# Six buffers of rounded weights moved to six different starts within 256 bytes

## The chip, the cores and the metric

The kernel runs on 1 core of a Trainium2 chip. The metric is the device time of one execution in microseconds; the median of three executions is quoted, and one further execution was recorded by the hardware profiler.

## What is computed

One residual decoder block on 512 tokens of width 2048, in fp32. Each sub-layer is normed and modulated by six vectors (shift, scale, gate, twice) that come from a conditioning vector `c`:

```python
mod = einsum('bd,de->be', silu(c), w_ada) + b_ada
h   = rms_norm(x, norm1) * (1 + sc1) + sh1
u, v, xb, gb = split(einsum('bsd,de->bse', h, w_in))
ya  = gmlp_spatial_gating(gelu(u), gelu(v), ...)
yb  = rg_lru(causal_dwconv(xb), ...) * gelu(gb)
mix = concat([rms_norm(ya), rms_norm(yb)])
x   = x + g1 * einsum('bse,ed->bsd', mix, w_out)
h   = rms_norm(x, norm2) * (1 + sc2) + sh2
gate, val = split(einsum('bsd,df->bsf', h, w_up))
x   = x + g2 * einsum('bsf,fd->bsd', gelu(causal_dwconv(gate)) * val, w_down)
out = rms_norm(x, norm_final)
```

The four weight products (`w_in`, `w_out`, `w_up`, `w_down`) are nearly all of the work.

## The kernel before

Weights arrive in blocks of 256 rows by 512 columns, each a tile of 128 partitions by 2 by 512 floats, 4096 bytes in each partition (`raw`, `rawb` or `t`). TensorE multiplies in fp32r. To keep fp32 precision, each weight block and each activation is held as two fp32r tiles: the rounded value, and the rest that rounding left out. Three matmuls then make one product: rounded times rounded, rounded weight times the activation's rest, and the weight's rest times the rounded activation.

The work is a list of 516 steps, one for each weight block. At step j, `round_step(j + 2)` has ScalarE cast the block of step j + 2 into a tile `wh` (`round_up`, L161 to L164) and `rest_step(j + 2)` has VectorE subtract it from the raw block into a tile `wl` (`rest`, L166 to L169); then TensorE runs the matmuls of step j. So weights are rounded two steps ahead, and three buffers of each kind (`WBUFS = 3`) turn over: one in use, one ready, one being written. The order of every engine's work is written out by hand (a manual schedule), with other work attached to steps by `put`.

Two kinds of step matter here. In 208 of them (`mm_w`, L171 to L176, and `mm_h`, L178 to L183) a step has 24 matmuls of 512 columns, in threes; each loads its own 128 x 128 stationary tile. In `mm_w` that tile is a slice of `wh` or `wl`, and the activation (`hp`, `dp`, `xs`) streams; in `mm_h` it is the other way round. The other 308 steps (`product`, L904 to L922) compute most of the up projection by a scheme of seven products of half size: each step has 8 pairs, one matmul of 512 columns with a slice of `wh` (L921) and one of 256 columns with a slice of `wl` (L922).

SBUF has two stacks of pools. The pool `weights` with the six buffers is the lowest of the left stack; above it stand in turn `mid`, `early`, `late`, `spare`, `ffn` and `back`, with `araw`, `yl`, `rawb`, `t`, `ht`, `la`, `dp` and others. The right stack (`main`) holds `hp`, `raw`, `xs` and constants. In the built program the six buffers start at bytes 1152, 5248 and 9344 (`wh`) and 13440, 17536 and 21632 (`wl`) of a partition. All six leave a remainder of 128 when divided by 256, and so do `hp`, `xs`, `dp`, `raw`, `rawb`, `t`, `yl` and most other large tiles. The constant tile `ones` starts at a remainder of 32; `ht`, `wst`, `wr`, `wi` and, in the stretch of the recurrent unit, `la` and `lc` start at 192 (`la` of a later pool also at 0); the four `araw` tiles at 128, 160, 192 and 224.

Of the kernel before, what the change touches and what calls it, by code (L numbers as in the profile page):

```python
# [9 lines left out]
F32 = mybir.dt.float32  # L10
F32R = mybir.dt.float32r
# [4 lines left out]
P = 128  # L16
S = 512
# [14 lines left out]
NMM = 6  # L32
NXS = 24
WBUFS = 3


ROUNDS = [(0, 2), (2, 6), (6, 10), (10, 16)]
# [13 lines left out]
def tile_block(ctx, tc, x_t, vec, w_ada, w_in, w_r, w_i, ws_t, w_out, w_up, w_us, w_dn, out):  # L51
# [3 lines left out]
    wts = ctx.enter_context(tc.tile_pool(name="weights", bufs=1))  # L55
# [5 lines left out]
    def sb(tag, bufs, shape=(P, S), dt=F32, pl=pool):  # L61
        count[0] += 1
        return pl.tile(list(shape), dt, name=f"{tag}_{count[0]}", tag=tag, bufs=bufs)
# [94 lines left out]
            put(j, fn, cost, half)  # L158


    def round_up(raw):  # L161
        hi = sb("wh", WBUFS, (P, 2, S), F32R, wts)
        A.copy(hi, raw)  # L163
        return hi  # L164

    def rest(raw, hi):  # L166
        lo = sb("wl", WBUFS, (P, 2, S), F32R, wts)
        V.tensor_tensor(out=lo, in0=raw, in1=hi, op=SUB)  # L168
        return [(hi[:, kk, :], lo[:, kk, :]) for kk in range(2)]  # L169

# [98 lines left out]
    def round_step(j):  # L269
        if j < len(steps):  # L270
            if j in source:
                raws[j] = source[j]()
            his[j] = round_up(raws[j])

    def rest_step(j):
        if j < len(steps):
            ws[j] = rest(raws.pop(j), his.pop(j))
# [1021 lines left out]
```

## Time and profile before

| | |
|---|---|
| median of 3 executions | 2104.73 us (2103.9 to 2104.93) |
| the profiled execution | 2104.92 us, of which the span from first to last instruction is 2103.2 us |
| granted TensorE clock, mean | 0.993 of full speed |
| TensorE matmul busy | 2069.0 us (98%), 10160 instructions |
| TensorE weight load busy | 1727.6 us (82%), 10160 instructions |
| VectorE busy | 1492.9 us (71%) |
| ScalarE busy | 923.8 us (44%) |
| GpSimd busy | 79.7 us (4%) |

Busy time of an engine is the sum of its instructions' durations, overlaps counted once. Matmuls are pipelined: a matmul's recorded duration includes the time in which its successor already streams, so the pace of TensorE is read from the distance between starts, not from durations.

### The profile page before, as it was taken

To read this page: it belongs to the slowest core of one execution; us is meant where nothing else is said; L and a number is where in the kernel's file an instruction comes from. 1 tells how busy PE (TensorE), PEld (TensorE's weight loads), DVE (VectorE), ACT (ScalarE), POOL (GpSimd) and SP (SyncE) were. 2 spreads that over 40 slices of the span, in tenths; PEclk is the share of its full clock that TensorE was granted. 3 is DMA by queue.
4 is the path that set the end of the run, shared out by engine and by line. 5 is a ranking of instruction groups with operands and counts; after the bars stand their busy time and mean duration, and the time that the engine had idled before them with its cause. 6 is when DMAs were issued, how large, how long until landed. Compare 5 with 4: busy or idle time off the path is not lost.

```text
span 2103.2 us, 26309 instructions
## 1 busy us (share of the span) xinstructions
PE 2069.0 (98%) x10160; PEld 1727.6 (82%) x10160; DVE 1492.9 (71%) x1865; ACT 923.8 (44%) x1165; POOL 79.7 (4%) x100
## 2 busy tenths in 40 slices
PE   7999999999989999999999999999999999999997
PEld 4887777888868888888888888888888888888886
DVE  8999889788767888888888888888875223432333
ACT  5323666332234555555555555555553222322223
POOL 0000000000000000000000000000000000000000
PEclk9999999999999999999999999999999999999999
DMA  9977434589825677877877867767755334423222
GB/s 374 327 288 264 141 127 154 199 296 367 298 95 159 212 225 202 241 216 202 242 216 204 240 211 210 248 198 235 216 177 199 121 119 141 159 91 99 92 90 100
DMA packets 116061, 420.36 MB, mean 200 GB/s; under 512 B 14816, under 2 KB 14944, under 8 KB 103648
## 3 DMA queue, kind: packets, MB, share of 16 engines
q1 hardware_dynamic: 87280, 315.39, 42.6%
q0 software_dynamic: 12672, 46.14, 11.6%
q10 hardware_dynamic: 15984, 57.15, 7.9%
q8 instruction: 80, 1.31, 0.2%
q14 instruction: 45, 0.37, 0.0%
HBM read 397.66 MB, written 20.97 MB: 199 GB/s over the span
## 4 chain that ended last, share of the span: by engine, by line
PE 87%; DVE 7%; ACT 3%; issue 1%; DMA 1%; SPq 0%; ACTq 0%; DVEq 0%
PE mm L921 28%; PE mm L922 14%; PE mm L174 13%; PE mm L175 13%; PE mm L176 13%; DVE araw L212 2%; PE mm L181 1%; PE mm L183 1%; PE mm L182 1%; DVE wl L168 1%; DMA araw<-w_ada 1%; DVE xs L359 1%; PE sm L655 0%; DVE la L685 0%; DVE xs L734 0%
## 5 line engine op out<-in xcount | busy, mean ns | idle before, releaser
L163 ACT CAST wh<-raw 128x1024 fp32r<-128x1024 f32 x296 | 311.7, 1053 | 615.1 <-PE mm L175 443.1
L168 DVE TENSOR_TENSOR wl<-raw,wh 128x1024 fp32r<-128x1024 f32 x296 | 360.9, 1219 | 303.8 <-ACT wh L163 303.4
L921 PE MATMUL mm<-hp,wh 128*128 128x512 f32 x1408 | 499.5, 399 | 0.0
L174 PE MATMUL mm<-hp,wh 128*128 128x512 f32 x1184 | 469.0, 396 | 6.7 <-ACT hp L229 5.8
L175 PE MATMUL mm<-hp,wh 128*128 128x512 f32 x1184 | 463.6, 392 | 0.5 <-DVE hp L237 0.5
L176 PE MATMUL mm<-hp,wl 128*128 128x512 f32 x1184 | 462.8, 391 | 0.0
L922 PE MATMUL mm<-hp,wl 128*128 128x256 f32 x1408 | 395.4, 281 | 0.0
L921 PE MATMUL mm<-xs,wh 128*128 128x512 f32 x1056 | 375.1, 399 | 0.0
L921 PEld LDWEIGHTS mm<-hp,wh 128*128 128x128 f32 x1408 | 264.6, 188 | 66.1
L922 PE MATMUL mm<-xs,wl 128*128 128x256 f32 x1056 | 296.6, 281 | 0.0
L174 PEld LDWEIGHTS mm<-hp,wh 128*128 128x128 f32 x1184 | 223.7, 189 | 58.3 <-ACT hp L229 8.7
L922 PEld LDWEIGHTS mm<-hp,wl 128*128 128x128 f32 x1408 | 266.0, 189 | 0.0
L175 PEld LDWEIGHTS mm<-hp,wh 128*128 128x128 f32 x1184 | 223.6, 189 | 50.1 <-issue 2.4
L176 PEld LDWEIGHTS mm<-hp,wl 128*128 128x128 f32 x1184 | 223.6, 189 | 46.6
L168 DVE TENSOR_TENSOR wl<-rawb,wh 128x1024 fp32r<-128x1024 f32 x176 | 214.9, 1221 | 65.6 <-ACT wh L163 65.6
L921 PEld LDWEIGHTS mm<-xs,wh 128*128 128x128 f32 x1056 | 198.4, 188 | 49.6
L922 PEld LDWEIGHTS mm<-xs,wl 128*128 128x128 f32 x1056 | 199.5, 189 | 0.0
L163 ACT CAST wh<-rawb 128x1024 fp32r<-128x1024 f32 x176 | 185.2, 1052 | 23.9 <-PE mm L921 13.3
L212 DVE SCALAR_TENSOR_TENSOR araw<-araw,crow 128x2050 f32<-128x2050 f32 (+1 forms) x80 | 182.6, 2286 | 2.5 <-DMA araw<-w_ada 2.4
L950 POOL DMA_DIRECT2D raw<-w_us x88 | 75.9, 862 | 1240.8 <-DMA rawb<-w_us 457.8
L974 ACT COPY u<-mm 128x512 f32<-128x512 f32 x88 | 51.7, 587 | 161.5 <-PE mm L922 161.5
L168 DVE TENSOR_TENSOR wl<-t,wh 128x1024 fp32r<-128x1024 f32 x44 | 53.9, 1225 | 50.3 <-ACT wh L163 50.3
(233 smaller groups left out, 2106.3 us busy)
## 6 DMA issues: line engine op xcount, KB each, us to landing
rawb<-w_us SPq DMA_DIRECT2D x132, 512.0 KB, 6.8
araw<-w_ada SPq DMA_DIRECT2D x48, 1024.5 KB, 7.6
raw<-w_dn SPq DMA_DIRECT2D x96, 512.0 KB, 3.6
raw<-w_us SPq DMA_DIRECT2D x88, 512.0 KB, 6.2
raw<-w_us POOLq DMA_DIRECT2D x88, 512.0 KB, 7.3
araw<-w_ada SPq DMA_DIRECT2D x32, 1025.0 KB, 8.4
raw<-w_in ACTq DMA_DIRECT2D x59, 512.0 KB, 4.6
yl<-w_ada SPq DMA_DIRECT2D x16, 1024.5 KB, 5.4
```

The costliest lines, as they stand in the source:

```text
L163: A.copy(hi, raw)
L168: V.tensor_tensor(out=lo, in0=raw, in1=hi, op=SUB)
L174: PE.matmul(ps, w[0][:, cs], h[0], start=first, stop=False)
L175: PE.matmul(ps, w[0][:, cs], h[1], start=False, stop=False)
L176: return PE.matmul(ps, w[1][:, cs], h[0], start=False, stop=last)
L181: PE.matmul(ps, h[0][:, cs], w[0], start=first, stop=False)
L182: PE.matmul(ps, h[0][:, cs], w[1], start=False, stop=False)
L212: V.scalar_tensor_tensor(out=raw, in0=raw, scalar=1.0, in1=crow[:, :w], op0=MUL, op1=MUL, accum_out=mods[:, n:n + 1])
L921: PE.matmul(both, hi[:, cs], m, start=first, stop=False, skip_group_check=True)
L922: PE.matmul(ps[:, lower], lo[:, cs], m[:, 0, :], start=False, stop=last, skip_group_check=True)
L950: G.dma_start(o[name], w_us[f - PLAIN, i], accum_op=ADD)
L974: A.copy(t, o["x"])
```

## The change

Each of the six buffers gets a tag of its own, in the same rotation by threes, and ahead of the first use of five of them a small pad tile is taken from the same pool: 8, 8, 8, 8 and 16 floats, that is 32, 32, 32, 32 and 64 bytes. The two kinds are first taken alternately, so that they now alternate in SBUF.

```diff
+PADS = {"wh": (0, 8, 8), "wl": (8, 8, 16)}
...
+    turn = {"wh": 0, "wl": 0}
+
+    def weight(kind):
+
+        i = turn[kind]
+        turn[kind] += 1
+        if i < WBUFS:
+            n = PADS[kind][i]
+            if n:
+                wts.tile([P, n], F32, name=f"pad_{kind}{i}")
+        return sb(f"{kind}{i % WBUFS}_", 1, (P, 2, S), F32R, wts)
+
     def round_up(raw):
-        hi = sb("wh", WBUFS, (P, 2, S), F32R, wts)
+        hi = weight("wh")
         A.copy(hi, raw)
         return hi

     def rest(raw, hi):
-        lo = sb("wl", WBUFS, (P, 2, S), F32R, wts)
+        lo = weight("wl")
         V.tensor_tensor(out=lo, in0=raw, in1=hi, op=SUB)
```

In the built program the buffers now start at these bytes (remainder of 256 behind each):

| buffer | before | after |
|---|---|---|
| `wh` 0 | 1152 (128) | 1152 (128) |
| `wl` 0 | 13440 (128) | 5280 (160) |
| `wh` 1 | 5248 (128) | 9408 (192) |
| `wl` 1 | 17536 (128) | 13536 (224) |
| `wh` 2 | 9344 (128) | 17664 (0) |
| `wl` 2 | 21632 (128) | 21824 (64) |

Everything above them in the left stack moves up by the 192 bytes of the pads: `rawb`, `t`, `dp`, `yl` and the tiles beside them go from a remainder of 128 to 64, `ht` and `la` from 192 to 128, the four `araw` tiles from 128, 160, 192, 224 to 64, 96, 128, 160. The right stack (`hp`, `xs`, `raw`) stays. The instructions of every engine stand in the same order as before, with the same kinds of waits.

## Rows read from the trace of the kernel before

**Rows 1.** The page: span, busy time of each engine, and TensorE's granted clock in 40 slices.
```profile
span 2103.2 us, 26309 instructions
PE 2069.0 (98%) x10160; PEld 1727.6 (82%) x10160; DVE 1492.9 (71%) x1865; ACT 923.8 (44%) x1165; POOL 79.7 (4%) x100
PEclk9999999999999999999999999999999999999999
```
**Rows 2.** Busy time in three stretches of 60 us (instructions counted if any part lies inside).
```profile
core 0: us, PE busy (x) PEld busy (x) DVE busy (x) ACT busy (x) POOL busy (x), PEclk, DMA share, GB/s
120.00:180.00 60.00, 60.00 (x267) 49.69 (x266) 55.91 (x67) 15.34 (x17) 0.00 (x0) 1.00 0.77 269
1620.00:1680.00 60.00, 60.00 (x267) 49.69 (x266) 18.61 (x20) 13.87 (x16) 0.00 (x0) 1.00 0.37 121
720.00:780.00 60.00, 60.00 (x342) 51.99 (x341) 49.72 (x55) 33.22 (x40) 5.17 (x6) 1.00 0.77 232
```
**Rows 3.** Instructions in order of time, down projection: start us, duration us, engine, line.
```profile
1700.16 0.39 PE L174 MATMUL mm<-xs,wh 128*128 128x512 f32 x1
1700.16 0.19 PEld L175 LDWEIGHTS mm<-xs,wh 128*128 128x128 f32 x1
1700.39 0.39 PE L175 MATMUL mm<-xs,wh 128*128 128x512 f32 x1
...
1703.79 0.39 PE L175 MATMUL mm<-hp,wh 128*128 128x512 f32 x1
```
**Rows 4.** The same view in the up projection.
```profile
1000.05 0.40 PE L921 MATMUL mm<-hp,wh 128*128 128x512 f32 x1
1000.29 0.28 PE L922 MATMUL mm<-hp,wl 128*128 128x256 f32 x1
1000.29 0.19 PEld L921 LDWEIGHTS mm<-hp,wh 128*128 128x128 f32 x1
1000.41 0.40 PE L921 MATMUL mm<-hp,wh 128*128 128x512 f32 x1
...
1002.17 0.40 PE L921 MATMUL mm<-hp,wh 128*128 128x512 f32 x1
```
**Rows 5.** Weight loads by line: out<-streamed,stationary; count; busy us, mean ns.
```profile
L921 PEld LDWEIGHTS mm<-hp,wh 128*128 128x128 f32 x1408 | 264.6, 188 | 66.1
L174 PEld LDWEIGHTS mm<-hp,wh 128*128 128x128 f32 x1184 | 223.7, 189 | 58.3 <-ACT hp L229 8.7 <-issue 2.4 <-DVE xs L359 1.3
L921 PEld LDWEIGHTS mm<-xs,wh 128*128 128x128 f32 x1056 | 198.4, 188 | 49.6
L655 PEld LDWEIGHTS sm<-la,wi 128*128 128x128 f32 x16 | 3.0, 189 | 3.8 <-issue 3.1 <-PE mm L183 0.5 <-ACT lc L657 0.3
L136 PEld LDWEIGHTS sm<-ones,xs 128*128 128x128 f32 x8 | 1.0, 192 | 0.0
L129 PEld LDWEIGHTS sm<-wst,ones 128*128 128x128 f32 x4 | 0.8, 190 | 1.0 <-issue 1.0
```
**Rows 6.** Pairs of fp32 matmuls in order of time, merged (x2: start, length of both).
```profile
209.01 1.02 PE L655 MATMUL sm<-la,wi 128*128 128x512 f32 x2
247.03 1.02 PE L129 MATMUL sm<-ht,ones 128*128 128x512 f32 x2
1857.84 1.02 PE L129 MATMUL sm<-xs,ones 128*128 128x512 f32 x2
```
**Rows 7.** One line's durations, ns min/median/max: the two tiles that VectorE takes at L212.
```profile
L212 DVE SCALAR_TENSOR_TENSOR araw<-araw,crow x80: 2262/2286/2296, 18.5 to 570.9; 128x2049 f32<-128x2049 f32 x48, 128x2050 f32<-128x2050 f32 x32
L212 DVE SCALAR_TENSOR_TENSOR yl<-yl,crow x16: 2284/2287/2292, 742.3 to 1474.4; 128x2049 f32<-128x2049 f32 x16
```
**Rows 8.** Groups by line: VectorE subtractions and 512-wide operations, ScalarE's cast.
```profile
L168 DVE TENSOR_TENSOR wl<-raw,wh 128x1024 fp32r<-128x1024 f32 x296 | 360.9, 1219 | 303.8 <-ACT wh L163 303.4
L1006 DVE TENSOR_TENSOR fg<-gw 128x512 f32<-128x512 f32 x44 | 30.0, 681 | 0.0
L663 DVE TENSOR_TENSOR lc<-lc,la 128x512 f32<-128x512 f32 x8 | 5.4, 686 | 6.8 <-ACT lc L657 6.8
L253 DVE TENSOR_TENSOR sqs<-sqs,la 128x512 f32<-128x512 f32 x9 | 6.2, 691 | 0.7
L163 ACT CAST wh<-raw 128x1024 fp32r<-128x1024 f32 x296 | 311.7, 1053 | 615.1 <-PE mm L175 443.1 <-issue 67.1 <-PE mm L183 51.9
```
**Rows 9.** The chain of waits: its shares of the span by line.
```profile
by line: PE mm L921 27.5%; PE mm L922 13.9%; PE mm L174 13.1%; PE mm L175 13.1%; PE mm L176 13.0%; DVE araw L212 1.9%; PE mm L181 1.4%; PE mm L183 1.4%; PE mm L182 1.4%; issue 1.2%; DVE wl L168 1.1%; DMA araw<-w_ada 0.8%; DVE xs L359 0.5%; 
```

## The prediction

> **What bounds the kernel now.** The page comes first: TensorE's matmuls are busy for 98% of a span of 2103.2 us, VectorE for 71%, ScalarE for 44%, and the granted clock reads 9 in all 40 slices [rows 1]. The chain of waits says the same from the other side: lines 921, 922, 174, 175, 176, 181, 182 and 183, the matmuls on weights, hold 27.5 + 13.9 + 13.1 + 13.1 + 13.0 + 3 x 1.4 = 84.8% of the span [rows 9]. So a change of data placement counts only where it changes the pace of TensorE, or where it makes another engine so slow that TensorE waits for it.
>
> A recorded matmul runs into its successor, so the pace is read from starts. In the down projection 15 matmuls of 512 columns lie between the start at 1700.39 and that at 1703.79 us: 3.40 / 15 = 0.2267 us each [rows 3]. In the up projection six pairs (512 columns with `wh`, 256 with `wl`) lie between 1000.05 and 1002.17 us: 0.3533 us a pair [rows 4]. With the counts of the code, 208 steps of 24 matmuls take 208 x 24 x 0.2267 = 1132 us and 308 steps of 8 pairs take 308 x 8 x 0.3533 = 871 us, together 2003 of the 2103 us; the other 100 are start-up and waits.
>
> The clock in these stretches is granted in full [rows 2], that is 2.4 GHz. If a column takes one cycle (my estimate of the floor), 512 columns take 213.3 ns and 512 + 256 take 320.0 ns. So 13.4 ns of each single matmul and 33.3 ns of each pair are not columns: 4992 x 13.4 = 67 us and 2464 x 33.3 = 82 us, 149 us in all. That excess is the only thing on the path that a buffer's start could plausibly change, and the question of this case is whether it depends on the start.
>
> **The change, part by part.** No instruction is added, removed or moved; the pads are never written. What moves is where five of the six weight buffers start (one stays at a remainder of 128), and with them, by 192 bytes, everything else in the left stack.
>
> *TensorE disturbed by the other engines.* Were TensorE slowed when ScalarE or VectorE touch buffers at the same remainder, its pace would depend on how busy they are. Between 120 and 180 us VectorE is busy for 55.91 of 60 us, between 1620 and 1680 us for 18.61; `wh` and `wl` are written and read alike in both. TensorE starts the same 267 matmuls in each, with the same 49.69 us of weight loads [rows 2]. Term: 0.
>
> *TensorE's own two readings.* A weight load reads 512 bytes per partition of a buffer while the matmul before it streams its activation. In all fp32r matmuls both sides start at a remainder of 128, so no row shows one at another remainder; this price has to be bounded by neighbours. The fp32 matmuls have them: `la` with `wi` (both 192), `ht` (192) with `ones` (32), `xs` (128) with `ones` (32). Each pair of equal length is 1.02 us long, whether the two remainders agree or not [rows 6]. Those matmuls stream at half the pace, so they could hide a small effect. The loads themselves take 188 to 189 ns from `wh` at 128, 189 from `wi` at 192, 190 from `ones` at 32, and 192 in the longest group, whose tile is `xs` at 128 again [rows 5]. A load for a matmul of 512 columns begins with the matmul before it and has 0.23 us of cover [rows 3, 4]: for those a few ns are hidden. The load at L921 is the one without cover: it begins at 1000.29 us beside the 256-column matmul, and its own matmul starts at 1000.41, before the load's recorded end [rows 4]. There are 2464 of them, and two of the three `wh` buffers move, so 1643 loads count. Two ns either way (190 against 188) make 3.3 us. I take 0, the value of the nearest row (189 at 192 against 188 at 128, within rounding), and keep -3.3 and +3.3 for the range.
>
> *VectorE and ScalarE.* The subtraction into `wl` takes 1219 ns and the cast into `wh` 1053 ns [rows 8]. VectorE's 512-wide operations take 681 ns with all tiles at 128, 686 with all at 192, and 691 where 128 meets 192 or 0 [rows 8]: a spread of 10 ns with no plain order. On the big product at L212 four different starts give 2262 to 2296 ns about a median of 2286, one start at 128 gives 2287 [rows 7]. Doubled for 1024 columns that is 20 ns for each subtraction. Even in the tightest stretch a step lasts 24 x 0.2267 = 5.44 us, so 11 of them fit into 60 us, and 11 x 20 ns = 0.22 us goes into 60 - 55.91 = 4.09 us of idle time [rows 2]. Term: 0; were that cover gone, 0.4 us over the 100 us of that stage. ScalarE, busy for 15.34 of 60 us there, hides the same for its cast.
>
> *Transfers.* `araw`, `rawb` and `dp` tiles land or are written 64 bytes further down within 256. Of transfers only those into `araw` are in the chain, with 0.8% of the span, 17 us [rows 9]; they already land at four different starts. An estimate of 1% of these 17 us is 0.2 us either way. Term: 0.
>
> **Sum.** 0 against the profiled execution's 2104.92 us (span 2103.2 and 1.7 around it); that execution lies 0.2 us above the median of the runs, 2104.73. Prediction: 2104.7 us.
>
> **A rule against the row.** The rows give 226.7 ns from start to start at 512 columns and full clock [rows 3]. The Trainium skill, in TensorE: Matmul & The Clock Gate, section Wait — 56ns, not 53.3ns?, states that back-to-back matmuls at full clock start N / 2.4 GHz plus about 2.5 ns apart, 215.7 ns at 512. The trace does not agree; by that rule 11.0 ns of each single matmul and 28.4 of each pair are a disturbance of this kernel, 125 us in all, and if the shared start were its cause the time would fall towards 1980 us. The same skill, in SBUF — State Buffer, section Who interferes with whom, says that TensorE never waits on another engine for SBUF; by that nothing could come back, and rows 2 agree with it.
>
> **The rivals.**
>
> *Faster: the excess is a collision of starts.* The weight load and the streamed activation both begin at a remainder of 128 today; if they step through SBUF in such a way that they meet, five of six buffers would now miss the stream. All of their share would be 149 x 5/6 = 124 us: 1981 us. Three per cent of the excess (4.2 of 149 us) is enough to be seen as faster. For it: 13.4 ns are there on every matmul, unexplained. Against it: equal and different remainders give the same 1.02 us in fp32 [rows 6], and the excess is the same in every stage, whatever streams and whoever else works [rows 2, 3].
>
> *Slower: the weight load pays for its new start.* Place: the uncovered loads at L921, from `wh` 1 and `wh` 2. If they take the 192 ns of the longest group instead of 188 [rows 5], 1643 x 4 ns = 6.6 us lie on the path: 2111.3 us. It decides from 4.2 us / 1643 = 2.6 ns for each load on. Against it: the 192 ns belong to a tile at 128, so they are not the price of another remainder.
>
> *The change does not do what it says.* The starts in the built program are the six that are promised, so this rival could only be that the shift of the rest undoes it; the streamed tiles `dp` now start at 64 while `hp` and `xs` stay at 128. It would give 2104.7 us too.
>
> **How the numbers follow.** A difference of 0.2%, 4.2 us, is about what a measurement of this kernel can tell from no change. No effect on the path: 0.81. The faster rival: 0.11, above the slower because there is an unexplained excess of 149 us to draw from. The slower rival: 0.08. The range is that of the likeliest case: 2104.7, less and plus the uncovered loads' 3.3, the transfers' 0.2, VectorE's 0.4 and 0.5 for the spread of the three runs, so 2100.3 to 2109.1 us; it leaves out the two rivals, 0.19 together.
>
> **What would show it.** If I am right, the start-to-start distances in the changed kernel are again 0.2267 and 0.3533 us, the 60-us stretches hold the same counts of matmuls, and the subtraction and the cast stay within 10 ns of 1219 and 1053. The faster rival would show as distances nearer 0.213 and 0.320 us in both kinds of step; the slower one only in the pairs, as more than 0.355 us, with longer loads at L921. A gap in front of a matmul that waits for ScalarE's cast or VectorE's subtraction would mean that the cover I named was too thin. I am wrong if the median leaves 2100.3 to 2109.1 us.

## The result and the profile after

The change made the kernel slower: 2118.43 us median (2117.91 to 2119.02, 4 runs) against 2104.41 us (2103.9 to 2104.93, 4 runs) for the kernel before in the same series, a ratio of 1.0066 with a 95% interval of 1.0052 to 1.008. The prediction, 2104.7 us in a range of 2100.3 to 2109.1, was wrong.

The page of the changed kernel, to be held against [rows 1]:

```profile
span 2117.3 us, 26309 instructions
PE 2085.8 (99%) x10160; PEld 1727.4 (82%) x10160; DVE 1495.3 (71%) x1865; ACT 920.3 (43%) x1165; POOL 80.7 (4%) x100
PEclk9999999999999999999999999999999999999999
```

The span grew by 14.1 us and TensorE's busy time by 16.8. The same instructions, at the same granted clock, keep TensorE busy for longer, and waits shrink by a little. The time of all weight loads together has not changed (1727.4 against 1727.6 us). So what grew lies neither in waits nor in the loads' own durations.

Where TensorE lost its time shows in the three stretches of [rows 2], here of the changed kernel, in the same columns:

```profile
120.00:180.00 60.00, 60.00 (x260) 48.56 (x259) 54.14 (x67) 15.30 (x17) 0.00 (x0) 1.00 0.77 262
1620.00:1680.00 60.00, 60.00 (x260) 48.51 (x259) 19.00 (x22) 13.62 (x15) 0.00 (x0) 1.00 0.38 123
720.00:780.00 60.00, 60.00 (x345) 52.54 (x344) 50.43 (x55) 32.92 (x40) 4.29 (x5) 1.00 0.71 211
```

In the two stretches of triples 60 us hold 260 matmuls instead of 267; in the stretch of pairs they hold 345 instead of 342. The change has two effects of opposite sign. Triples became slower, whether VectorE is busy (54.14 of 60 us) or not (19.00), and pairs became faster.

The single starts, in order of time, answer to [rows 3] and [rows 4]. The names of `wh` and `wl` now keep their numbers, because each buffer has a tag of its own.

```profile
1700.81 0.39 PE L187 MATMUL mm<-xs,wh__2350_14066 128*128 128x512 f32 x1
...
1703.59 0.40 PE L187 MATMUL mm<-xs,wh__2350_14066 128*128 128x512 f32 x1
```

Twelve matmuls take 2.78 us, 0.2317 us each instead of 0.2267. In the up projection:

```profile
1000.14 0.39 PE L934 MATMUL mm<-xs,wh__1339_7954 128*128 128x512 f32 x1
...
1002.22 0.39 PE L934 MATMUL mm<-xs,wh__1339_7954 128*128 128x512 f32 x1
...
1002.56 0.40 PE L934 MATMUL mm<-xs,wh__1342_7978 128*128 128x512 f32 x1
...
1003.97 0.40 PE L934 MATMUL mm<-xs,wh__1342_7978 128*128 128x512 f32 x1
```

Six pairs of one step take 2.08 us, 0.347 us each; four pairs of the next step, which has the next buffers, take 1.41 us, 0.3525 each. Before, pairs had 0.3533 in the mean, whatever the buffer's turn (0.352 to 0.354). The pace now goes by buffer.

Sorting all matmuls of the two traces by their buffers' starts, from start to start and without those behind a gap, gives this:

| | before | after, `wh`/`wl` at 128/160 | at 192/224 | at 0/64 |
|---|---|---|---|---|
| a triple, stream `hp` at 128 | 680.5 ns | 699.3 ns | 694.9 ns | 699.8 ns |
| a pair, stream at 128 | 353.3 ns | 346.1 ns | 353.2 ns | 348.2 ns |

Summed over the kernel, triples went from 0.9 to 27.3 us above 680 ns each, pairs fell by 10.3 us, and what distances of over 260 ns hold beyond a normal one, the waits, shrank from 25.4 to 23.4 us. Together 26.4 - 10.3 - 2.0 = 14.1 us, the growth of the span. The small net time hides two larger effects.

### The profile page after: what moved, and what is told of

Same layout as the page of the kernel before. It is cut to its first block, busy times and chain, and to the rows that moved or that the text cites. A ratio compares the mean times of both kernels' runs of the same rounds, so it can differ in the third digit from the quotient of the medians.

```text
span 2117.3 us, 26309 instructions
## 1 busy us (share of the span) xinstructions
PE 2085.8 (99%) x10160; PEld 1727.4 (82%) x10160; DVE 1495.3 (71%) x1865; ACT 920.3 (43%) x1165; POOL 80.7 (4%) x100
## 4 chain that ended last, share of the span: by engine, by line
PE 92%; DVE 4%; ACT 2%; DMA 1%; issue 1%; SPq 0%; ACTq 0%; DVEq 0%
PE mm L934 27%; PE mm L187 14%; PE mm L188 14%; PE mm L189 14%; PE mm L935 14%; PE mm L194 2%; PE mm L195 2%; PE mm L196 2%; DVE araw L225 1%; DMA raw<-w_in 0%; PE sm L130 0%; PE sm L668 0%; DVE xs L747 0%; ACT xs L1125 0%; PE sm L187 0%
## 5 line engine op out<-in xcount | busy, mean ns | idle before, releaser
L856 DVE SCALAR_TENSOR_TENSOR fy<-fg,vt,fy 128x511 f32<-128x511 f32 x88 | 65.9, 749 | 1.5
L1021 ACT ACTIVATE fy<-fg,vt 128x512 f32<-128x512 f32 x44 | 36.0, 817 | 44.2 <-DVE fg L1019 44.2
L979 DVE TENSOR_TENSOR rawb<-rawb,t 128x1024 f32<-128x1024 f32 x44 | 53.7, 1220 | 0.0
L976 DVE TENSOR_TENSOR t<-rawb,raw 128x1024 f32<-128x1024 f32 x44 | 53.6, 1219 | 0.0
L1009 DVE TENSOR_TENSOR vw<-mm,u 128x512 f32<-128x512 f32 x44 | 30.4, 690 | 20.2 <-ACT u L987 20.2
L372 DVE TENSOR_TENSOR xs<-mm,xs 128x512 f32<-128x512 f32 x60 | 38.9, 686 | 4.1 <-PE mm L189 3.7
L225 DVE SCALAR_TENSOR_TENSOR yl<-yl,crow 128x2049 f32<-128x2049 f32 x16 | 36.6, 2289 | 0.0
L1028 DVE TENSOR_TENSOR fy<-fy,vw 128x512 f32<-128x512 f32 x44 | 30.5, 693 | 4.4
L1001 DVE TENSOR_TENSOR gw<-mm,c 128x512 f32<-128x512 f32 x44 | 30.2, 686 | 0.0
L1024 DVE SCALAR_TENSOR_TENSOR vw<-vw 128x512 f32<-128x512 f32 x44 | 30.1, 685 | 0.0
L1015 DVE TENSOR_TENSOR vw<-mm,u 128x512 f32<-128x512 f32 x44 | 30.1, 684 | 0.0
L248 DVE TENSOR_TENSOR hp<-ht,hp 128x512 fp32r<-128x512 f32 x16 | 10.8, 691 | 16.8 <-ACT hp L240 16.8
```

What stands on the lines that cost most here:

```text
L225: V.scalar_tensor_tensor(out=raw, in0=raw, scalar=1.0, in1=crow[:, :w], op0=MUL, op1=MUL, accum_out=mods[:, n:n + 1])
L856: V.scalar_tensor_tensor(out=y[:, i:], in0=src[:, :S - i], scalar=taps(f)[2 - i], in1=y[:, i:], op0=MUL, op1=ADD)
L976: V.tensor_tensor(out=o["P6"], in0=o["P3"], in1=o["P5"], op=ADD)
L979: V.tensor_tensor(out=o["P2"], in0=o["P2"], in1=o["P6"], op=ADD)
```

## The experiments

Four theories stood at the start. **A**: the starts of the weight tiles set TensorE's pace, through the load meeting the stream or the loads meeting each other. **B**: a load costs more where it begins at an odd multiple of 32 bytes. **C**: it is the new order of the buffers, `wh` and `wl` in turn. **D**: it is the shift of everything above them.

### Order alone, shift alone, starts alone

Tags of their own without pads:

```diff
-PADS = {"wh": (0, 8, 8), "wl": (8, 8, 16)}
+PADS = {"wh": (0, 0, 0), "wl": (0, 0, 0)}
```

> A tag of its own for each of the six buffers and the alternating order, but no pads: all six at a remainder of 128, the stack above where it was. Theory A (the remainders of the weight tiles set TensorE's pace): 2104 us, starts 0.2267 us apart at 512 columns and 0.3533 us a pair. Theory C (that wh and wl now alternate, 4 KB apart, is what counts): 2118 us, triples of 0.694 to 0.700 us.

Measured: 2105.89 us against 2105.09, ratio 1.0003 (0.9993 to 1.0012). The order costs nothing that can be told from zero; C falls.

The kernel before, with the shift above alone:

```diff
         lo = sb("wl", WBUFS, (P, 2, S), F32R, wts)
+        if not above:
+            above.append(wts.tile([P, 48], F32, name="pad_above"))
```

> The six buffers as in the kernel before, and one pad of 192 bytes behind them: only the tiles above move (dp, rawb, araw and the rest). Theory A: 2104 us, the paces of before, perhaps with a change in the 352 triples and 32 token triples that use dp. Theory D (the shift of the rest of the stack costs the time): 2118 us.

Measured: 2108.43 us, ratio 1.0015 (1.0006 to 1.0025). Not 2118, so D falls as the main cause, but there is a small cost, and its place is clear: triples that stream `dp`, now at 64 beside loads at 128, take 700.1 ns instead of 680.6, and triples in which `dp` is loaded 695.6 instead of 681.1, 3.6 us over all. In the stretch from 1960 to 2000 us, where `dp` streams in part of the triples, 184 matmuls are counted instead of 186. All other triples and the pairs keep their pace.

The change, with the stack above put back:

```diff
-        return sb(f"{kind}{i % WBUFS}_", 1, (P, 2, S), F32R, wts)
+        t = sb(f"{kind}{i % WBUFS}_", 1, (P, 2, S), F32R, wts)
+        if kind == "wl" and i == WBUFS - 1:
+            wts.tile([P, 16], F32, name="pad_above")
+        return t
```

> The change, with another 64 bytes of pad behind the six buffers, so that the tiles above are back at their remainders of before. Theory A: 2118 us and triples of 0.694 to 0.700 us in the first 1550 us. Theory D: 2104 us.

Measured: 2119.02 us, ratio 1.0068 (1.0051 to 1.0085), with the triples and pairs of the changed kernel. The six starts are the cause, and the shift above adds nothing visible to them; A or B.

### TensorE by itself

```python
def single(a, s, n):        # rem a: of the load, s: of the stream
    for i in range(n):
        PE.matmul(ps[i % 4], at(wa, a, i % 4 * P, P), at(hh, s, 0, S), start=True, stop=True)
...
for s in REM:
    for a in REM:
        single(a, s, 32)
```

> Nothing of the block is computed; the output is the input x. TensorE alone runs fp32r matmuls from one rounded tile per operand, sliced at chosen remainders of 256: single matmuls of 512 columns for all 64 combinations of the start of the load and of the stream, then triples (same slice twice, then a slice of a second tile) and pairs (512 and 256 columns) for all 64 combinations of the two loads' starts with the stream at 128. Theory A in the form that the load meets the stream: the distance of starts depends on the difference of the two remainders alone, with 0.2267 us at equal starts. Theory B (a load that starts at an odd multiple of 32 costs more): it depends on the load's start alone, and is longer at 32, 96, 160 and 224. If neither holds and it is the two loads of a triple that matter, single matmuls are flat at 0.2267 us, and triples vary with the difference of the loads' starts.

Merged rows of 21 single matmuls (start, length of all, count), first with load and stream both at 128, then with the load at 192, then both at 64, then the load at 128 on a stream at 64:

```profile
284.70 4.93 PE L52 MATMUL ps<-hh,wa 128*128 128x512 f32 x21
299.49 5.06 PE L52 MATMUL ps<-hh,wa 128*128 128x512 f32 x21
151.03 4.93 PE L52 MATMUL ps<-hh,wa 128*128 128x512 f32 x21
165.83 5.06 PE L52 MATMUL ps<-hh,wa 128*128 128x512 f32 x21
```

Without the last matmul's own 0.39 or 0.40 us, 20 distances make 4.54 or 4.66 us: 0.227 us where the remainders are equal, 0.233 where the load is 64 bytes past the stream, and that alike for streams at 128 and at 64. Over all 64 combinations the distance goes by the difference (load minus stream) with no more than 2 ns between streams (without the first matmuls of the program, which start 427 ns apart):

| difference, bytes | 0 | 32 | 64 | 96 | 128 | 160 | 192 | 224 |
|---|---|---|---|---|---|---|---|---|
| ns, start to start, stream at 128 | 226.6 | 233.3 | 233.3 | 234.2 | 233.4 | 233.1 | 228.8 | 233.4 |

From 40 us on nothing but TensorE runs here, so no other engine has a part in it. B falls: a load at 160 has 226.6 ns on a stream at 160. What is left of A is that a load pays by its distance from the stream beside it, and the equal start, which the faster rival took for a collision, is the cheap one. Of triples, 64 combinations of the two loads' starts on a stream at 128 give 680.0 ns at (128, 128) and 686 to 707 elsewhere; of pairs, 346 to 354. One value did not fit: pairs at (128, 128) had 346.7 ns here, and 353.3 in the kernel.

### All at another start, and all moved together

Six buffers at 192, everything else where it was:

```diff
+    wts.tile([P, 16], F32, name="pad_below")
...
         lo = sb("wl", WBUFS, (P, 2, S), F32R, wts)
+        if not above:
+            above.append(wts.tile([P, 48], F32, name="pad_above"))
```

> All six buffers at one remainder, 192, with the streams and the rest of the stack where they were (128). Theory A2 (a load costs nothing extra only where it starts at the remainder of the stream beside it): triples with the weights as stationary tile 700 ns as at (192, 192) in the map of starts, token triples about 687, pairs unchanged at 353: 1440 x 20 + 224 x 7 ns = 30 us more, 2135 us. Theory A1 (it is the spread of the six among themselves that costs): 2104 us.

Measured: 2130.88 us, ratio 1.0122 (1.0107 to 1.0137). Triples 700.0 ns, token triples (`mm_h`, where the activation is loaded and the weight streams) 688.2 with `hp` and 687.3 with `dp`, pairs 353.3, all as forecast; 28.1 us more in triples and 2.9 us less in gaps make 25.2 of the span's 24.6. The time is 4 us below the forecast, which counted no shorter gaps and 2 us more in triples. A stretch of triples and one of pairs:

```profile
1620.00:1680.00 60.00, 60.00 (x259) 48.35 (x258) 21.02 (x24) 15.69 (x19) 0.00 (x0) 1.00 0.42 136
720.00:780.00 60.00, 60.00 (x342) 52.09 (x341) 49.72 (x55) 32.96 (x40) 4.30 (x5) 1.00 0.70 208
```

So the spread of the six among themselves is not needed: one common start, 192 beside streams at 128, is worse than the six.

Buffers and streamed tiles all at 64:

```diff
+    wts.tile([P, 48], F32, name="pad_below")
...
+    pool.tile([P, 16], F32, name="pad_end")
     own.__exit__(None, None, None)
```

> The six buffers and the streamed tiles (hp, xs, dp) all at a remainder of 64 instead of 128. Theory A2: only the difference counts, so 2104 us, triples of 680 ns and pairs of 353 ns. If 128 itself were the good start: 2118 us or more.

Measured: 2104.95 us against 2104.59, ratio 0.9999 (0.9989 to 1.0008), triples 680.5, pairs 353.3. At 64 as at 128, only the difference counts.

### The two halves of the change

The six starts in one kind of step alone (the second kernel has `if j in source`, which picks the steps of pairs):

```diff
+STARTS = {"wh": (0, 16, 32), "wl": (8, 24, 48)}
...
+    def place_at(kind, j):
+        o = STARTS[kind][j % WBUFS] if j not in source else 0
+        t = sb(kind, WBUFS, (P, 2 * S + 64), F32R, wts)
+        return t[:, o:o + 2 * S].rearrange("p (a b) -> p a b", a=2)
...
-        hi = sb("wh", WBUFS, (P, 2, S), F32R, wts)
+        hi = place_at("wh", j)
```

> The six starts of the change (128, 192, 0 for wh; 160, 224, 64 for wl) in the 208 steps of triples alone; in the 308 steps of pairs all at 128, as before; the rest of the stack at its remainders. If the two kinds of step are independent terms: 27 us more in the triples, some 2 of them covered by shorter waits, pairs at 353.3 ns: 2130 us. If the terms depend on each other: something else.

> The other half: the six starts in the 308 steps of pairs alone, all at 128 in the triples. If independent: triples at 680 ns, pairs 346.1, 353.2 and 348.2 ns by buffer, 10 us less: 2094 us.

Measured: in pairs alone 2095.41 us, ratio 0.9952 (0.9935 to 0.9968), as forecast. In triples alone 2113.92 us, ratio 1.0042 (1.0027 to 1.0057), 16 us below the forecast. The stretches (first two of triples, third of pairs) of the kernel with the starts in triples alone:

```profile
120.00:180.00 60.00, 60.00 (x260) 48.54 (x259) 54.13 (x67) 15.29 (x17) 0.00 (x0) 1.00 0.76 262
1620.00:1680.00 60.00, 60.00 (x260) 48.43 (x259) 17.15 (x18) 12.58 (x13) 0.00 (x0) 1.00 0.36 114
720.00:780.00 60.00, 60.00 (x348) 52.45 (x347) 49.93 (x54) 33.35 (x41) 4.88 (x6) 1.00 0.72 218
```

and of the other:

```profile
120.00:180.00 60.00, 60.00 (x267) 49.67 (x266) 55.91 (x69) 15.34 (x17) 0.14 (x1) 1.00 0.78 271
1620.00:1680.00 60.00, 60.00 (x266) 49.67 (x266) 15.05 (x15) 11.60 (x11) 0.00 (x0) 1.00 0.39 123
720.00:780.00 60.00, 60.00 (x345) 52.48 (x345) 50.31 (x56) 33.45 (x41) 5.15 (x6) 1.00 0.78 232
```

The triples fell out as expected (260 and 267). But the first kernel's pairs, with every start at 128 as before, hold 348 matmuls, not 342: they run at 346.7 ns, and 2464 x 6.66 ns = 16.4 us are most of what is missing, 17.8 us in the profiled execution (2112.19 us). The same remainders have two paces. The four executions fall into two groups (2112.19 and 2112.38, 2115.47 and 2115.62 us); only the first execution was profiled, so what the pairs did in the slower two is not known.

### What a pace depends on besides

> Nothing of the block is computed; the output is the input x. TensorE alone: single matmuls of 512 columns with the load 0 to 252 bytes past the stream's remainder in steps of 4, and 256 to 4096 bytes past it; of 256 and 128 columns in steps of 32; and pairs with the second load at 128 or 160, with one or four PSUM banks, accumulating or not, with the output and the streamed tile as one run of 512 or two of 256. Theory A2 with a period of 256 bytes: 226.6 ns at 0 and at every multiple of 256, 228.8 to 234.2 in between, with no step at multiples of 32 alone. If the block of 16 or 32 bytes counts: plateaus of that width. Pairs: one of the forms, the one that the kernel has, gives 353.3 ns at (128, 128) where the plain form gave 346.7.

Measured, single matmuls: 226.7 ns at 0, 256, 512, 768, 1024, 2048 and 4096 bytes past the stream: multiples of 256 bytes count as equal, which fits a period of 256. Between, no plateaus of 16 or 32 bytes: about 233 at most differences, up to about 237 at 164, but also 226.7 at 100, 120, 132, 144, 156, 228 and 252. For 128 columns the distance is 111.7 ns at all eight differences tried; for 256 columns it is 116.7 to 120.0, and 120.0 at the equal start, so there the equal start is not the fast one. Pairs with both loads at 128, written (128, 128), had 353.3 ns in all seven forms, the plain form of the first probe among them, and pairs at (128, 160) 346.8: the form is not what tells this probe from the first.

> Nothing of the block is computed; the output is the input x. TensorE alone, stream at 128: 64 pairs with both loads at 128, each time after 32 pairs with the second load at another remainder, then the same for the second load at 160, then triples with all at 128 after triples with the third load elsewhere. If the pace at given starts is fixed, every block at (128, 128) has one value. If it also depends on the rhythm that TensorE came from, (128, 128) shows 346.7 ns after some and 353.3 after others, as the two maps did; triples at 128 come back to 680 ns after all.

Measured: after pairs with the second load at 32, 64 or 192, and after triples, pairs at (128, 128) took 353.3 ns; after 0, 96, 128, 160 or 224 they took 346.7. In the kernel before, too, pairs come behind triples with all at 128, and have 353.3. Seven pairs' starts after 32, then after 160, with all operands at 128 in both:

```profile
69.76 0.40 PE L65 MATMUL ps<-hh,wa 128*128 128x512 f32 x1
...
71.88 0.40 PE L65 MATMUL ps<-hh,wa 128*128 128x512 f32 x1
```

```profile
203.65 0.39 PE L65 MATMUL ps<-hh,wa 128*128 128x512 f32 x1
...
205.73 0.39 PE L65 MATMUL ps<-hh,wa 128*128 128x512 f32 x1
```

2.12 / 6 = 0.3533 us, 2.08 / 6 = 0.3467 us. Each holds for its whole block of 64 pairs. Pairs at (128, 160) took 346.5 to 346.8 ns after all eight predecessors, and triples at 128 came back to 680.0 after all.

> Nothing of the block is computed; the output is the input x. TensorE alone: 32 single matmuls with the load 0, 12, 24, ... 252 bytes past the stream, each block after 24 matmuls at one of three starts (0, 64 or 160 past the stream). If the pace of singles is a matter of the start alone, the three rows agree at every start. If it also depends on the rhythm before, they differ at some starts; at 0 all are expected at 226.7 ns, since triples came back to 680 ns after every predecessor.

Measured: at 0 the distance is 226.7 ns after each of the three. At 72, 84, 96 and 108 bytes past the stream, at 192 and at 204 it hardly depends on what came before (about 229 to 236). At 120 and 132 it is 226.7 after all three. At 12, 36, 144, 216, 228 and 252 it stays at 226.7 after equal starts, and is 230.7 to 234.5 after the two others; 156 has 226.7 after two of the three and about 244 after the third. So a good rhythm, a pace of 226.7 ns once it runs, can be kept at some starts that would not find it by themselves.

### A version that beats both

The kernel before, with the rest tile `wl` 32 bytes further on in the pair steps alone:

```diff
+APART = 8
...
-    def rest(raw, hi):
-        lo = sb("wl", WBUFS, (P, 2, S), F32R, wts)
+    def rest(raw, hi, off):
+        t = sb("wl", WBUFS, (P, 2 * S + 64), F32R, wts)
+        lo = t[:, off:off + 2 * S].rearrange("p (a b) -> p a b", a=2)
...
-            ws[j] = rest(raws.pop(j), his.pop(j))
+            ws[j] = rest(raws.pop(j), his.pop(j), APART if j in source else 0)
```

> The kernel before, with wl tiles 256 bytes larger: in the 308 steps of pairs the rest is written and read 32 bytes into its tile (remainder 160), in the 208 steps of triples at its start (128). If a load's remainder against the stream's sets the pace, triples stay at 680 ns and pairs come to the 346.1 ns that buffers 128 and 160 have in the changed kernel: 2464 x 7.2 ns = 17.7 us less, 2087 us. If the pace of a pair depends on the turn of six different starts, or on something else that moved, 2104 us.

Measured: 2088.03 us against 2104.59, ratio 0.992 (0.9903 to 0.9936). Its page and two of its stretches, triples and pairs:

```profile
span 2086.4 us, 26309 instructions
120.00:180.00 60.00, 60.00 (x266) 49.69 (x266) 55.90 (x69) 15.34 (x17) 0.61 (x2) 1.00 0.80 271
720.00:780.00 60.00, 60.00 (x349) 52.51 (x348) 50.76 (x55) 32.31 (x40) 5.16 (x6) 1.00 0.77 233
```

Triples keep 680.6 ns, all pairs have 346.7, and 2464 x 6.66 ns = 16.4 us come back, which is the 16.6 measured. In the history probe this pace did not hang on the pairs that came before. 680 and 346.7 ns are, to half a nanosecond, the least that any probe showed, so no start that was tried gives more.

## Why the prediction was wrong

*What bounds the kernel* held: TensorE's pace decides, and the decomposition into 4992 single matmuls and 2464 pairs is the one in which the result adds up.

*TensorE disturbed by the other engines*, term 0: held. Triples lost the same 7 matmuls in 60 us with VectorE busy and idle, and TensorE alone shows the same effect.

*TensorE's own two readings*, term 0 with bounds of 3.3 us: this step failed, in three places. First, the neighbour: I took the fp32 matmuls for proof that remainders do not matter, and set aside that they stream at half the pace; fp32r matmuls of 512 columns at seven other multiples of 32 bytes took 2 to 8 ns longer. Second, the way of pricing: I looked at the durations of loads, and asked which are covered. Loads did not get longer in sum (1727.4 against 1727.6 us); the distance between matmuls did, also in the triples, which were taken for covered because a load of 0.19 us ends before its matmul starts [rows 3]. Third, the bound: with 1643 loads of 2 ns it left out the 4992 matmuls in which the cost arose. The term measured +26.4 us in triples, 5.3 ns per matmul, and -10.3 us in pairs. Its sources also hold more than was read from them: the 192 ns are not the longest group of loads, since the listing has `mm<-xs,ones` at 322 and `sm<-ht,ones` at 209 ns, both at L129. That touches the slower rival's price alone.

*VectorE and ScalarE*, term 0: held. All 516 subtractions and all 516 casts of the changed kernel, in the view of busy time by line over the span:

```profile
0.00:2117.00 2117.00, 631.39 (x516) 0.99 0.62 199
0.00:2117.00 2117.00, 541.61 (x516) 0.99 0.62 199
```

are 1224 and 1050 ns each, within 5 ns of 629.64 / 516 = 1220 and 543.04 / 516 = 1052 before.

*Transfers*, term 0: held for the transfers, as far as the span adds up without them, but the shift of the stack was not free. I gave the streamed tile `dp` one clause and no price; by itself that shift costs 3.3 us, as the kernel with the shift alone shows; beside the six starts it costs nothing visible (2118.43 us with it, 2119.02 without). The transfers into `araw` were not the only ones in the chain: one of `hp<-x_t` held 6.11 us there, which changes nothing in the sum.

*The faster rival* had the mechanism's place (load beside stream) and, for singles and triples, its sign backwards: no start was cheaper there than the equal one. Only pairs gave time back. Of its 149 us of excess, 67 us on singles stay at every start tried, and 16.4 of 82 on pairs can be had, without giving up the equal start in triples. The 215.7 ns of the Trainium skill (TensorE: Matmul & The Clock Gate, section Wait — 56ns, not 53.3ns?) are not reached: no block of 512-column fp32r matmuls came below 226.6 here. *The slower rival* had the right sign and the wrong place: it waited for longer pairs, and pairs became shorter; that its 2111.3 us lies nearest to the measured time is luck. That the excess was "the same in every stage" was no evidence against a dependence on starts, because every fp32r operand of the kernel before began at the same remainder.

What stays open is the cause inside the chip. The Trainium skill, in TensorE: Matmul & The Clock Gate, section Step-by-step: what each phase is for, says that loading the next weights does not take SBUF read bandwidth from the running matmul. No run here measures that bandwidth, but the two are not independent: with TensorE alone, the load's start moves the pace from 226.6 to 234.2 ns. That the two readings meet in SBUF would fit the dependence on their difference and the period of 256 bytes, and was not shown. Why a rhythm, once found, persists was not tried either.

## What to carry to other kernels

Where fp32r matmuls of 512 columns bound the time, give the tile that is loaded and the tile that is streamed the same start within 256 bytes, and check it in the built program after any change of pools: 64 bytes of difference cost 3% of the pace of triples here. It is no rule for every stream of matmuls: pairs of 512 and 256 columns gained 2% with the second load 32 bytes further on, and whether a start is good has to be tried for each pattern. Read TensorE's pace from start to start, by buffer, not from durations of loads or from its busy share. Where all operands happen to agree, a trace can't say what disagreement costs; try it with TensorE alone before pricing it at zero.

## What the runs showed that was not expected

For single matmuls of 512 columns and for triples equal starts are fast, and differences are not graded: singles have 226.7 ns at 0 and at a few other differences, and mostly 233.3 elsewhere. The pace of pairs has two stable values at the same addresses, 346.7 and 353.3 ns, chosen by the matmuls that came before and kept for a whole block in the probe; in each profiled kernel with all pairs at one start, one pace held for all 2464 pairs. The kernel with the six starts in its triples alone thereby got better pairs. So a change in one stage can move the pace of the next, with no wait between them.
